# RWKV preparation of an encoder block: the next pair's k projection between the parts of a pair, the norm sums ahead of the bonus, low-rank products over 128 rows

## The chip, the cores and the metric

One core of a Trainium2 chip runs the whole kernel, one layer of a hybrid encoder block on 1024 tokens of width 1024. The metric is the device time of one execution in microseconds. The engines are TensorE (PE; its weight loads are PEld), VectorE (DVE), ScalarE (ACT) and GpSimd (POOL); SyncE (SP) issues most of the DMAs. Each engine works through its own instructions in order, and they wait for each other by semaphores.

## The reference

The block projects the normed input once, runs windowed attention and a bidirectional RWKV-7 scan on parts of the projection, joins them, and ends with an MLP and a gated embedding. The change touches only what is computed ahead of the RWKV scan:

```python
zr = proj[..., O_RWKV:O_GATE]
zr = zr + shift_mu[i] * (centred_shift(zr) - zr)
...
r, k, v = z[..., :c], z[..., c:2 * c], z[..., 2 * c:3 * c]
w_raw = (w0[:, None, None, :] + jnp.einsum('btr,drc->dbtc', jnp.tanh(wl), w2)).astype(f32)
decay = jnp.exp(-jnp.exp(-jax.nn.softplus(-w_raw) - 0.5))
a = jax.nn.sigmoid((a0[:, None, None, :] + jnp.einsum('btr,drc->dbtc', al, a2)).astype(f32))
kk = (k * k_k).astype(f32).reshape(bsz, t, *hn)
kk = kk / jnp.maximum(jnp.sqrt(jnp.sum(kk * kk, axis=-1, keepdims=True)), 1e-12)
k_dir = (k.astype(f32)[None] * (1.0 + (a - 1.0) * k_a.astype(f32))).reshape(2, bsz, t, *hn)
...
bonus = jnp.einsum('bthn,dbthn,dhn->bth', rh, k_dir, r_k.astype(f32))[..., None] * vh
```

There are 8 heads of 64, two directions d, and low ranks of 64 for w2 and a2. r, k and v each have 512 columns.

## The kernel before

**Stages.** Norm of the input and q, k, v of the attention; the RWKV preparation; then attention, the chunks of the scan, the output projection and the MLP, which this change leaves as they are. Every product in float32 is made of three matmuls of rounded parts: a high part, and a low part that is the remainder. `split` (L187, L188) makes the two: a cast on ScalarE and a subtraction on VectorE, or on GpSimd for weights. `load_w` loads 128 columns of weights in two parts (`wst`), and splits them into `whi` and `wlo`, two buffers deep.

**A pair.** The preparation goes over four pairs of heads, p = 0 to 3; a tile holds the 128 channels of a pair by all 1024 tokens. For each pair come three projections of 48 matmuls (two halves of 512 tokens, 8 blocks of k, 3 products). `shifted` evacuates one: two copies per half from PSUM on ScalarE (`zr`, `z`), a sum of the two neighbours on GpSimd (`sm`) and one operation on VectorE that ends `z`. PSUM holds two halves of a projection (`mm`, two buffers), so a third half waits for the evacuation of the first. `z` has four buffers; `zr` and `sm` have one, and `ri` shares that of `sm`.

**The norm.** `sq` is the square of k on ScalarE; `sums2` splits it and sums over a head with a matmul by a block of ones; `ri` is the larger of the sum and a small number, then Ln and Exp on ScalarE (L636, L637), each with a load of its table; `kk` is k times it. **The directions.** `lora` makes a low-rank product: two halves, each one matmul with the high weights (L547) and one with the low ones (L548), then tanh on ScalarE. The operand `lr` holds its high part in 64 rows and its low part in the other 64, so that one matmul of 128 rows does two of the three products; the low weights need only 64 rows. From the decay product come a scan over the chunks (L644), `E` and `Ei` (exponentials), `Dt`, and `ra`, half of it on GpSimd; from the rate product come `kd`, `bk` and `rk`, and `ra` and `bk` are stored. rk of the second direction times r (L680) ends a pair on VectorE. **The bonus.** `add_bonus` splits rk, transposes v on PE (`vtp`), copies it out (`vt`, L584), sums rk over the heads and multiplies by v (`bv`). It belongs to pair p, and its steps are called within pair p + 1. `vt` and `bv` share one buffer.

**What sets the order.** A scheduler at compile time orders each engine's instructions by the order of the code and a model of costs, except where `keep_in_program_order` pins one. So the code places work roughly: `proj_with` calls hooks at given matmuls (`VH`) of the v projection: before the change the rest of the last bonus and the split of sq at matmul 8, the sums of the norm at matmul 23. In the last pair `fill0` puts matmuls of the branch gates (28 or 40 at a time, `gmm`) behind the low-rank products.

Of the kernel before, what the change touches and what calls it, by code (L numbers as in the profile page):

```python
# [9 lines left out]
F32 = mybir.dt.float32  # L10
F32R = mybir.dt.float32r
AF = mybir.ActivationFunctionType
ALU = mybir.AluOpType
# [4 lines left out]
P = 128  # L18
T = 1024
# [5 lines left out]
NP = 4  # L25
NH = 8
ND = 2
FF = 4096
PLE = 256
O_RWKV = 768  # L30
# [7 lines left out]
NFS = {2: "s0", 3: "c0 s1", 4: "t0 c1 t1 s2 c2", 5: "t2 s3 c3", 6: "t3 s4 c4", 7: "s5 c5"}  # L38
EXPIN = (1, 0)
EPS_AT = (3, 3, 2, 2)  # L40
VH = (8, 23)
TPAT = (1, 3)
HDAT = (1, 4, 6)
H6 = (4, 1)
# [93 lines left out]
def block_kernel(ctx: ExitStack, tc: tile.TileContext, I: dict, out: bass.AP):  # L138
    nc = tc.nc
# [23 lines left out]
    kT_d = DR.tile([P, 2, 2, T], F32R, name="kT_d")  # L163
# [131 lines left out]
    with ExitStack() as s0:  # L295
# [141 lines left out]
        for h in range(2):  # L437
            ps = PMM.tile([P, 512], F32, name="mm", tag="mm", bufs=2)
# [21 lines left out]
    sQ.close()  # L460

    kT = PY.tile([P, 2, 2, T], F32R, name="kT", tag="yk")
    nc.gpsimd.dma_start(kT, kT_d)
    gmask = const("gmask", [P, ND, P])
    pc = G.tile([P, NPC], F32, name="pc")
    nc.sync.dma_start(pc, I["pc"])
# [9 lines left out]
    with ExitStack() as s1:  # L476
# [19 lines left out]
        nc.vector.tensor_scalar(out=oka, in0=hka, scalar1=-1.0, scalar2=1.0, op0=ALU.mult, op1=ALU.add)  # L496

        wlr_h = [A1.tile([P, ND, 512], F32R, name=f"wlrh{i}") for i in range(2)]
        wlr_l = A1.tile([P, ND, 512], F32R, name="wlrl")
        hrows, lrows = [slice(0, 64), slice(64, 128)], [slice(64, 128), slice(0, 64)]  # L500
        for i in range(2):
            st = A1.tile([P, ND, 512], F32, name="wlrst", tag="th", bufs=2)
            for rows in hrows:
                nc.sync.dma_start(st[rows], I["wa2"][hrows[i]])
            nc.vector.tensor_copy(wlr_h[i], st)
            nc.vector.tensor_tensor(out=wlr_l[hrows[i]], in0=st[hrows[i]], in1=wlr_h[i][hrows[i]].bitcast(F32), op=ALU.subtract)
        scan = A1.tile([P, T], F32, name="scan")
        nc.sync.dma_start(scan, I["scan"])

# [31 lines left out]
        def lora(d, p, i, bias_col):  # L541

            th = A1.tile([P, T], F32, name="th", bufs=2)
            for h in range(2):
                ps = PX.tile([P, 512], F32, name="px", tag="px", bufs=6)
                cs_, hs = slice(p * P, (p + 1) * P), slice(512 * h, 512 * h + 512)
                nc.tensor.matmul(ps, wlr_h[i][:, d, cs_], lr[i][:, hs], start=True, stop=False)  # L547
                nc.tensor.matmul(ps, wlr_l[hrows[i], d, cs_], lr[i][hrows[i], hs], start=False, stop=True)  # L548
                nc.scalar.activation(out=th[:, 512 * h:512 * h + 512], in_=ps, func=AF.Tanh, scale=0.5, bias=hb[:, bias_col:bias_col + 1])
            return th  # L550

# [42 lines left out]
        def fill0(p, i):  # L594

            if p == NP - 1:
                for _ in range(F0[i]):
                    next(gates0)

        def proj_with(c0, hooks):  # L600
# [9 lines left out]
                    i += 1  # L610
            return pss

        bonus = None
        for p in range(NP):
            if bonus:
                next(bonus)
            kz = shifted(O_RWKV + 512 + p * P, 4 + p)
            rz = shifted(O_RWKV + p * P, p, pin=p > 0)

            kk = A1.tile([P, T], F32, name="kk", bufs=1)  # L620
            ri = A1.tile([P, T], F32, name="ri", tag="sm", bufs=1)
# [1 line left out]
            nc.scalar.activation(out=sq, in_=kz, func=AF.Square, scale=col("k_k", p))  # L623
            sums = sums2(one_r, sq)

            def after_bonus():
                if bonus:
                    next(bonus)
                next(sums)

            def norms():
                for hs, ps in next(sums):
                    nc.vector.tensor_scalar_max(ri[:, hs], ps, 1e-24)

            vz = shifted(O_RWKV + 1024 + p * P, 8 + p, proj_with(O_RWKV + 1024 + p * P, {VH[0]: after_bonus, VH[1]: norms}), pin=True)
            nc.scalar.activation(out=ri, in_=ri, func=AF.Ln)  # L636
            nc.scalar.activation(out=ri, in_=ri, func=AF.Exp, scale=-0.5)  # L637
            nc.vector.scalar_tensor_tensor(out=kk, in0=kz, scalar=col("k_k", p), in1=ri, op0=ALU.mult, op1=ALU.mult)
            for d in range(ND):
                th = lora(d, p, 0, d * NP + p)  # L640
                fill0(p, 2 * d)
                nc.scalar.activation(out=th, in_=th, func=AF.Identity, scale=W_SCALE, bias=wsc)
                sl = slice(None) if d == 0 else slice(None, None, -1)
                nc.vector.tensor_tensor_scan(out=th[:, sl], data0=scan, data1=th[:, sl], initial=0.0, op0=ALU.mult, op1=ALU.add)  # L644
                Lc = th.rearrange("p (c t) -> p c t", t=C)
                E = A1.tile([P, NCH, C + 1], F32, name="E", bufs=1)
                Ei = A1.tile([P, NCH, C], F32, name="Ei", bufs=1)
                if d == 0:
                    nc.vector.memset(E[:, :, 0:1], 1.0)
                    E1, E2, last = E[:, :, 0:C], E[:, :, 1:C + 1], C - 1  # L650
                else:
                    nc.vector.memset(E[:, :, C:C + 1], 1.0)
                    E1, E2, last = E[:, :, 1:C + 1], E[:, :, 0:C], 0
                nc.scalar.activation(out=E2, in_=Lc, func=AF.Exp)
                nc.scalar.activation(out=Ei, in_=Lc, func=AF.Exp, scale=-1.0)
                sl = slice(None) if d == 0 else slice(None, None, -1)
                nc.vector.tensor_copy(Dt[:, d, p, sl], E2[:, :, last])
                ra = A1.tile([P, NCH, 2, C], F32, name="ra", bufs=1)
                bk = A1.tile([P, NCH, 2, C], F32, name="bk", bufs=1)

                def ch(x):
                    return x.rearrange("p (c t) -> p c t", t=C)

                nc.vector.scalar_tensor_tensor(out=ra[:, :, 0, :], in0=ch(kk), scalar=-1.0, in1=E1, op0=ALU.mult, op1=ALU.mult)
                nc.gpsimd.tensor_tensor(out=ra[:, :, 1, :], in0=ch(rz), in1=E2, op=ALU.mult)
                ta = lora(d, p, 1, 8 + d * NP + p)
                fill0(p, 2 * d + 1)
                kd = A1.tile([P, T], F32, name="kd", bufs=1)
                nc.scalar.activation(out=kd, in_=ta, func=AF.Identity, scale=hka[:, p:p + 1], bias=oka[:, p:p + 1])
                nc.vector.tensor_tensor(out=kd, in0=kd, in1=kz, op=ALU.mult)  # L670
                nc.vector.scalar_tensor_tensor(out=ta, in0=ta, scalar=1.0, in1=kk, op0=ALU.add, op1=ALU.mult)
                bs, ks = (0, 1) if d == 0 else (1, 0)
                nc.vector.scalar_tensor_tensor(out=bk[:, :, bs, :], in0=ch(ta), scalar=0.5, in1=Ei, op0=ALU.mult, op1=ALU.mult)
                nc.vector.tensor_tensor(out=bk[:, :, ks, :], in0=ch(kd), in1=Ei, op=ALU.mult)
                if d == 0:
                    rk = A1.tile([P, T], F32, name="rk", bufs=1)
                    nc.vector.tensor_scalar_mul(rk, kd, col("r_k", p))
                else:
                    nc.vector.scalar_tensor_tensor(out=rk, in0=kd, scalar=col("r_k", NP + p), in1=rk, op0=ALU.mult, op1=ALU.add)
                    nc.vector.tensor_tensor(out=rk, in0=rk, in1=rz, op=ALU.mult)  # L680
                nc.sync.dma_start(ra_d[d, :, :, p, :].rearrange("c q x -> q c x"), ra.rearrange("q c a t -> q c (a t)"))
                nc.sync.dma_start(bk_d[d, :, :, p, :].rearrange("c q x -> q c x"), bk.rearrange("q c a t -> q c (a t)"))
            bonus = add_bonus(p, rk, vz)

        fill0(NP - 1, 4)
        for _ in bonus:
# [1107 lines left out]
```

## Time and profile before

| | |
|---|---|
| median of 3 runs | 1844.6 us (1842.85 to 1845.58) |
| the profiled execution | 1840.7 us |
| its span, first to last instruction | 1838.9 us |
| PE busy | 1726.5 us, 94% |
| VectorE busy | 1135.0 us, 62% |
| ScalarE busy | 880.4 us, 48% |
| GpSimd busy | 322.2 us, 18% |
| mean granted TensorE clock | 0.977 |
| the preparation's projections, k of pair 0 on PE | from 123.5 us |
| last rk product (L680) of pairs 0, 1, 2, 3 ends at | 201.6, 251.3, 301.8, 356.4 us |
| first attention scores on PE (L839) | 384.8 us |

A busy PE is not a PE at its peak: matmuls are pipelined, and one of 512 columns lasts 0.39 us while the next starts 0.23 us behind it. In rows of the timeline stand the start, the length, engine, line, operation, output and inputs; in square brackets stands how long the engine was idle before it, and what ended that. The share of the whole span says little of one stage, so the preparation is cut out by times.

### The profile page before, as it was taken

To read this page: it belongs to the slowest core of one execution; us is meant where nothing else is said; L and a number is where in the kernel's file an instruction comes from. 1 tells how busy PE (TensorE), PEld (TensorE's weight loads), DVE (VectorE), ACT (ScalarE), POOL (GpSimd) and SP (SyncE) were. 2 spreads that over 40 slices of the span, in tenths; PEclk is the share of its full clock that TensorE was granted. 3 is DMA by queue.
4 is the path that set the end of the run, shared out by engine and by line. 5 is a ranking of instruction groups with operands and counts; after the bars stand their busy time and mean duration, and the time that the engine had idled before them with its cause. 6 is when DMAs were issued, how large, how long until landed. Compare 5 with 4: busy or idle time off the path is not lost. (4 is left out here: it accounts for less than half of the span.)

```text
span 1838.9 us, 31199 instructions
## 1 busy us (share of the span) xinstructions
PE 1726.5 (94%) x12056; PEld 1414.7 (77%) x12056; DVE 1135.0 (62%) x1947; ACT 880.4 (48%) x1640; POOL 322.2 (18%) x265
## 2 busy tenths in 40 slices
PE   7999888999999899988889989999999999999998
PEld 7976666666677777776669978777877888888998
DVE  5645777745936555676563487666675777685432
ACT  5545666547754545556531245444343444554221
POOL 3453544531132121121132000000000000000000
PEclk9998999999999999999999989999999999999999
DMA  5462344674377474676564315544546874564111
GB/s 200 99 175 92 103 143 144 194 204 115 100 206 206 128 211 130 176 216 191 180 209 155 104 40 181 163 132 144 165 132 226 297 255 121 189 218 141 56 40 41
DMA packets 287125, 286.06 MB, mean 156 GB/s; under 512 B 49409, under 2 KB 203905, under 8 KB 286849
## 3 DMA queue, kind: packets, MB, share of 16 engines
q1 hardware_dynamic: 278720, 270.76, 47.7%
q0 software_dynamic: 7824, 12.59, 2.5%
q8 instruction: 95, 1.56, 0.4%
q10 hardware_dynamic: 432, 0.73, 0.1%
q14 instruction: 54, 0.43, 0.1%
HBM read 203.26 MB, written 80.74 MB: 154 GB/s over the span
## 5 line engine op out<-in xcount | busy, mean ns | idle before, releaser
L188 POOL TENSOR_TENSOR wlo<-wst,whi 128x512 fp32r<-128x512 f32 (+1 forms) x108 | 170.1, 1588 | 341.1 <-ACT whi L187 296.8
L1681 PE MATMUL ff2ps<-th,sh 128*128 128x512 f32 x448 | 174.2, 391 | 4.1 <-ACT th L187 4.1
L1681 PE MATMUL ff2ps<-tl,sh 128*128 128x512 f32 x448 | 175.0, 391 | 0.0
L1681 PE MATMUL ff2ps<-th,sl 128*128 128x512 f32 x448 | 174.9, 390 | 0.0
L175 POOL TENSOR_TENSOR rstd<-ms,neghalf 128x1 f32<-128x1 f32 x24 | 13.3, 554 | 813.8 <-DVE ms L173 813.8
L187 ACT CAST sh<-sst 128x512 fp32r<-128x512 f32 x109 | 67.8, 622 | 114.9 <-PE ff2ps L1681 72.0
L188 DVE TENSOR_TENSOR sl<-sst,sh 128x512 fp32r<-128x512 f32 x109 | 75.0, 688 | 52.5 <-ACT sh L187 52.3
L1681 PEld LDWEIGHTS ff2ps<-th,sh 128*128 128x128 f32 x448 | 84.2, 188 | 22.3 <-ACT th L187 4.5
L1681 PEld LDWEIGHTS ff2ps<-th,sl 128*128 128x128 f32 x448 | 84.5, 189 | 17.7
L1681 PEld LDWEIGHTS ff2ps<-tl,sh 128*128 128x128 f32 x448 | 84.5, 189 | 17.5
L187 ACT CAST whi<-wst 128x512 fp32r<-128x512 f32 (+1 forms) x108 | 68.9, 650 | 57.0 <-DMA wst<-in_w_in_dram 17.4
L187 ACT CAST w1h<-w1st 128x512 fp32r<-128x512 f32 x48 | 29.2, 614 | 102.3 <-DMA w1st<-in_w_ff_dram 101.7
L226 PE MATMUL plps<-wg,hp 128*128 128x256 f32 x256 | 73.5, 287 | 0.0
L228 PE MATMUL plps<-wg,hp 128*128 128x256 f32 x256 | 72.5, 283 | 0.0
L226 PE MATMUL mmo<-whi,mh 128*128 128x256 f32 x256 | 72.4, 283 | 0.0
L227 PE MATMUL plps<-wg,hp 128*128 128x256 f32 x256 | 72.4, 283 | 0.0
L228 PE MATMUL mmo<-whi,ml 128*128 128x256 f32 x256 | 72.1, 282 | 0.0
L227 PE MATMUL mmo<-wlo,mh 128*128 128x256 f32 x256 | 72.1, 282 | 0.0
L188 DVE TENSOR_TENSOR w1l<-w1st,w1h 128x512 fp32r<-128x512 f32 x48 | 32.7, 686 | 52.7 <-ACT w1h L187 52.7
L208 PE MATMUL gps<-rm,bkp 128*128 128x256 f32 x256 | 62.1, 385 | 2.3 <-ACT tm L1061 1.5
L1034 DVE TENSOR_TENSOR gm<-gps,gmask 128x512 f32<-128x512 f32 x64 | 43.7, 684 | 29.5 <-PE gps L208 29.5
L1757 ACT ACTIVATE pth<-plps 128x256 f32<-128x256 f32 x32 | 12.3, 385 | 101.6 <-PE plps L228 101.6
(399 smaller groups left out, 5190.4 us busy)
## 6 DMA issues: line engine op xcount, KB each, us to landing
wst<-in_w_in_dram SPq DMA_DIRECT2D x92, 256.0 KB, 3.6
tst<-in_w_ff_dram SPq DMA_DIRECT2D x80, 256.0 KB, 3.9
w1st<-in_w_ff_dram SPq DMA_DIRECT2D x32, 512.0 KB, 5.5
hid_S<-h SPq DMA_DIRECT2D x64, 256.0 KB, 2.1
sst<-hid_S SPq DMA_DIRECT2D x64, 256.0 KB, 2.7
hid_A<-h SPq DMA_DIRECT2D x48, 256.0 KB, 2.0
sst<-hid_A SPq DMA_DIRECT2D x45, 256.0 KB, 3.7
ra_d<-ra SPq DMA_DIRECT2D x8, 1024.0 KB, 4.5
```

Source lines behind the costliest of these rows:

```text
L175: nc.gpsimd.tensor_tensor(out=r, in0=ms, in1=neghalf.broadcast_to([P, width]), op=ALU.pow)
L187: a = nc.scalar.copy(hi, src)
L188: b = (lo_eng or nc.vector).tensor_tensor(out=lo, in0=src, in1=hi.bitcast(F32), op=ALU.subtract)
L208: tc.keep_in_program_order(nc.tensor.matmul(*a, **kw))
L226: nc.tensor.matmul(ps, ah, bh, start=(i == 0), stop=False)
L227: nc.tensor.matmul(ps, ah, bl, start=False, stop=False)
L228: nc.tensor.matmul(ps, al, bh, start=False, stop=(i == n - 1))
L1034: nc.vector.tensor_tensor(out=gm[d][:, s % NB, 4 * h:4 * h + 4, :], in0=ps.rearrange("p j q t -> p (j q) t"), in1=gmask[:, d, :].unsqueeze ...
L1681: nc.tensor.matmul(banks[bs][i], x_[:, isl], y_, start=fresh and p + j == 0, stop=p == NPR - 1 and j == 2, skip_group_check=True)
L1757: nc.scalar.activation(out=th[:, 256 * m:256 * m + 256], in_=ps_, func=AF.Tanh, scale=0.5)
```

## The change

1. **Order.** The k projection of pair p + 1 (`k_of`) is called between the decay product of direction 0 and its scan; its r projection (`r_of`) at the end of pair p. Before, both opened pair p + 1.
2. **Hooks.** In the v projection the split of sq comes at matmul 2 and the norm's sums at 18; the split of rk comes at 20 and the rest of the bonus at 38.
3. **Low-rank products.** Each of the two operands gets low weights of its own with 128 rows, of which 64 are filled with zeros on GpSimd (the high weights times 0). L548 becomes a matmul of 128 rows.
4. **Buffers.** `rk` takes the buffer of `vt` and `bv`. The load of kT on GpSimd's queue is called in pair 1 instead of ahead of the preparation.

```diff
-VH = (8, 23)
+VH = (2, 18, 20, 38)
...
     kT = PY.tile([P, 2, 2, T], F32R, name="kT", tag="yk")
-    nc.gpsimd.dma_start(kT, kT_d)
...
-        wlr_l = A1.tile([P, ND, 512], F32R, name="wlrl")
+        wlr_l = [A1.tile([P, ND, 512], F32R, name=f"wlrl{i}") for i in range(2)]
...
             nc.vector.tensor_copy(wlr_h[i], st)
-            nc.vector.tensor_tensor(out=wlr_l[hrows[i]], in0=st[hrows[i]], in1=wlr_h[i][hrows[i]].bitcast(F32), op=ALU.subtract)
+
+            nc.gpsimd.tensor_scalar_mul(wlr_l[i][lrows[i]], wlr_h[i][lrows[i]].bitcast(F32), 0.0)
+            nc.vector.tensor_tensor(out=wlr_l[i][hrows[i]], in0=st[hrows[i]], in1=wlr_h[i][hrows[i]].bitcast(F32), op=ALU.subtract)
...
-                nc.tensor.matmul(ps, wlr_l[hrows[i], d, cs_], lr[i][hrows[i], hs], start=False, stop=True)
+                nc.tensor.matmul(ps, wlr_l[i][:, d, cs_], lr[i][:, hs], start=False, stop=True)
...
+        def k_of(p):
+            return shifted(O_RWKV + 512 + p * P, 4 + p)
+
+        def r_of(p):
+            return shifted(O_RWKV + p * P, p)
+
         bonus = None
+        kz, rz = k_of(0), r_of(0)
         for p in range(NP):
-            if bonus:
-                next(bonus)
-            kz = shifted(O_RWKV + 512 + p * P, 4 + p)
-            rz = shifted(O_RWKV + p * P, p, pin=p > 0)
+            nkz = None
...
-            def after_bonus():
-                if bonus:
-                    next(bonus)
-                next(sums)
+            def step(g):
+                if g:
+                    next(g)
...
-            vz = shifted(O_RWKV + 1024 + p * P, 8 + p, proj_with(O_RWKV + 1024 + p * P, {VH[0]: after_bonus, VH[1]: norms}), pin=True)
+            vz = shifted(O_RWKV + 1024 + p * P, 8 + p, proj_with(O_RWKV + 1024 + p * P, {
+                VH[0]: lambda: next(sums), VH[1]: norms, VH[2]: lambda: step(bonus), VH[3]: lambda: step(bonus)}))
+            if p == 1:
+                nc.gpsimd.dma_start(kT, kT_d)
...
                 th = lora(d, p, 0, d * NP + p)
+                if p + 1 < NP:
+                    if d == 0:
+                        nkz = k_of(p + 1)
                 fill0(p, 2 * d)
...
-                    rk = A1.tile([P, T], F32, name="rk", bufs=1)
+                    rk = A1.tile([P, T], F32, name="rk", tag="vt", bufs=1)
...
             bonus = add_bonus(p, rk, vz)
+            if p + 1 < NP:
+                kz, rz = nkz, r_of(p + 1)
```

The scheduler makes of it the following. Rows are instructions in an engine's order; lines of the changed program lie some lines further down than those of before (L680 became L690, L644 became L654).

VectorE, from the end of pair 1 (the last product of rk with r, first row) to kk of pair 2, before the change; `s` and `s2l` are the low halves of a split, `z` is what `shifted` ends, `px` a sum in PSUM:

```order
L680 TENSOR_TENSOR rk<-rk,z 128x1024
L649 MEMSET E 128x16
L188 TENSOR_TENSOR s_1408<-rk,s_1408 128x512
L188 TENSOR_TENSOR s2l<-rk,s2h 128x512
L523 SCALAR_TENSOR_TENSOR z<-sm,hmu,z 128x1024
L513 MEMSET zr 128x1
L514 MEMSET zr 128x1
L188 TENSOR_TENSOR s_1408<-sq,s_1408 128x512
L188 TENSOR_TENSOR s2l<-sq,s2h 128x512
L588 TENSOR_TENSOR bv<-px,z 128x512 x2
L633 TENSOR_SCALAR ri<-px 128x512 x2
L638 SCALAR_TENSOR_TENSOR kk<-z,pc,ri 128x1024
```

The same stretch after the change, and two rows further:

```order
L690 TENSOR_TENSOR rk<-rk,z 128x1024
L188 TENSOR_TENSOR s_1410<-sq,s_1410 128x512
L188 TENSOR_TENSOR s2l<-sq,s2h 128x512
L514 MEMSET zr 128x1
L637 TENSOR_SCALAR ri<-px 128x512 x2
L188 TENSOR_TENSOR s_1410<-rk,s_1410 128x512
L188 TENSOR_TENSOR s2l<-rk,s2h 128x512
L515 MEMSET zr 128x1
L659 MEMSET E 128x16
L645 SCALAR_TENSOR_TENSOR kk<-z,pc,ri 128x1024
L524 SCALAR_TENSOR_TENSOR z<-sm,hmu,z 128x1024
L589 TENSOR_TENSOR bv<-px,z 128x512 x2
```

The halves of sq and ri now stand ahead of the halves of rk, `bv` stands behind kk and the z of v, ahead of the scan, and the z that stood between the halves (of r) has moved to the end of the pair.

VectorE behind the first scan of pair 2, before:

```order
L644 SCALAR_TENSOR_TENSOR th<-scan,th 128x1024
L670 TENSOR_TENSOR kd<-kd,z 128x1024
L657 COPY Dt<-E 128x16
L664 SCALAR_TENSOR_TENSOR ra<-kk,E 128x16x64
L671 SCALAR_TENSOR_TENSOR th<-th,kk 128x1024
```

and after:

```order
L654 SCALAR_TENSOR_TENSOR th<-scan,th 128x1024
L667 COPY Dt<-E 128x16
L674 SCALAR_TENSOR_TENSOR ra<-kk,E 128x16x64
L662 MEMSET E 128x16
L524 SCALAR_TENSOR_TENSOR z<-sm,hmu,z 128x1024
L514 MEMSET zr 128x1
L515 MEMSET zr 128x1
L680 TENSOR_TENSOR kd<-kd,z 128x1024
```

The z of the next pair's k (fifth row) now stands ahead of kd and all that follows; on GpSimd the sum that it reads stands behind that engine's half of `ra` and one `wlo`.

ScalarE at the norm, before:

```order
L517 COPY zr<-mm 128x512
L520 ACTIVATE z<-mm,omm 128x512
L636 ACT_TABLE_LOAD
L636 ACTIVATE ri<-ri 128x1024
L637 ACT_TABLE_LOAD
L637 ACTIVATE ri<-ri 128x1024
```

and after:

```order
L518 COPY zr<-mm 128x512
L521 ACTIVATE z<-mm,omm 128x512
L187 CAST s_1410<-rk 128x512
L187 CAST s2h<-rk 128x512
L643 ACT_TABLE_LOAD
L643 ACTIVATE ri<-ri 128x1024
L585 COPY vt<-vtp 128x512 x2
L644 ACT_TABLE_LOAD
L644 ACTIVATE ri<-ri 128x1024
```

The casts of rk and the two copies of v's transposes moved into the norm; the copies read what PE transposes 7 matmuls behind the low sums of the norm. Elsewhere: PE has, per pair, the v projection with 4 + 4 sums and 8 transposes, 4 low-rank matmuls, the next k, the other 12 low-rank matmuls, the next r. The matmuls with the low parts of sq stand 13 matmuls behind those with the high parts. GpSimd issues the load of kT at the same place as before, ahead of the first sum of the preparation, and the two fills with zeros stand behind it, each ahead of one of the first two sums. Behind the preparation every engine's order is the same as before.

## The prediction

> **What bounds the kernel now.** The change touches one stage, the RWKV preparation, so I cut the span by its pairs of heads: from the end of one pair's last rk product on VectorE (L680) to the next. The view of windows gives pairs 1, 2 and 3, and a stretch that is used further down.
>
> ```profile
> 201.55:251.33 49.78, 44.76 (x176) 33.24 (x176) 37.59 (x37) 32.07 (x46) 23.10 (x11) 0.97 0.45 137
> 251.33:301.77 50.44, 45.65 (x176) 33.78 (x176) 37.66 (x38) 32.11 (x47) 23.13 (x11) 0.93 0.45 136
> 301.77:356.39 54.62, 51.96 (x198) 38.69 (x199) 39.46 (x33) 34.70 (x51) 29.55 (x17) 0.94 0.52 157
> 168.00:176.00 8.00, 8.00 (x16) 4.66 (x16) 8.00 (x8) 3.42 (x4) 6.13 (x2) 0.50 0.11 33
> ```
>
> After each length stand the busy us (and counts) of PE, PEld, DVE, ACT and POOL, then granted clock, DMA share and GB/s. PE is busy 45 of 50 us and looks like the bound, but part of that is half clock. The other view, VectorE in order of time, shows a chain that closes on itself.
>
> ```profile
> 250.12 1.21 DVE L680 TENSOR_TENSOR rk<-rk,z 128x1024 f32<-128x1024 f32 x1
> ...
> 252.40 2.02 DVE L188 TENSOR_TENSOR s<-rk,s 128x512 fp32r<-128x512 f32 x1 [1.03 <-ACT s L187]
> 254.34 0.68 DVE L188 TENSOR_TENSOR s2l<-rk,s2h 128x512 fp32r<-128x512 f32 x1
> ...
> 257.82 1.29 DVE L588 TENSOR_TENSOR bv<-px,z 128x512 f32<-128x512 f32 x2 [0.39 <-DMA v_d<-vt]
> 261.73 1.29 DVE L633 TENSOR_SCALAR ri<-px 128x512 f32<-128x512 f32 x2 [2.62 <-PE px L570]
> 267.04 1.28 DVE L638 SCALAR_TENSOR_TENSOR kk<-z,pc,ri 128x1024 f32<-128x1024 f32 x1 [4.03 <-ACT ri L637]
> 271.35 1.29 DVE L523 SCALAR_TENSOR_TENSOR z<-sm,hmu,z 128x1024 f32<-128x1024 f32 x1 [3.02 <-POOL sm L522]
> 272.56 2.29 DVE L644 TENSOR_TENSOR_SCAN th<-scan,th 128x1024 f32<-128x1024 f32 x1
> ...
> 274.77 2.25 DVE L670 TENSOR_TENSOR kd<-kd,z 128x1024 f32<-128x1024 f32 x1
> 276.94 2.15 DVE L657 COPY Dt<-E 128x16 f32<-128x16 f32 x1
> 279.01 1.21 DVE L664 SCALAR_TENSOR_TENSOR ra<-kk,E 128x1024 f32<-128x1024 f32 x1
> 280.15 1.21 DVE L671 SCALAR_TENSOR_TENSOR th<-th,kk 128x1024 f32<-128x1024 f32 x1
> ...
> 284.22 2.28 DVE L644 TENSOR_TENSOR_SCAN th<-scan,th 128x1024 f32<-128x1024 f32 x1
> ...
> 288.23 3.19 DVE L670 TENSOR_TENSOR kd<-kd,z 128x1024 f32<-128x1024 f32 x1 [1.70 <-ACT E L654]
> ...
> 300.56 1.21 DVE L680 TENSOR_TENSOR rk<-rk,z 128x1024 f32<-128x1024 f32 x1
> ```
>
> VectorE sits idle almost only between L680 and the scan, where the norm is made: PE's sums (2.62), Ln and Exp (4.03), the sum of shifts on GpSimd (3.02). From 271 to 301 it waits once. So a pair has two parts: end of L680 (251.33) to end of the first scan (274.85), 23.5 us, mostly latency; and from there to the next L680 (301.77), 26.9 us, nearly solid VectorE work. The change reorders that ring, and I count it again in the new order.
>
> **First part, new order.** ScalarE's two steps, the three GpSimd groups and the memset come from these views (activities in order of time, one line's group, groups by form):
>
> ```profile
> 262.28 1.28 ACT L636 ACT_TABLE_LOAD   x1
> 263.58 1.06 ACT L636 ACTIVATE ri<-ri 128x1024 f32<-128x1024 f32 x1
> ```
> ```profile
> L584 ACT COPY vt<-vtp x8: 576/584/603, 203.5 to 366.1; 128x512 f32<-128x512 f32 x8
> ```
> ```profile
> L188 POOL TENSOR_TENSOR wlo<-wst,whi 128x512 fp32r<-128x512 f32 x43 | 74.8, 1749 | 85.9 <-ACT whi L187 85.9
> L522 POOL TENSOR_TENSOR sm<-zr 128x1024 f32<-128x1024 f32 x14 | 27.2, 1946 | 53.5 <-ACT zr L517 26.8 <-issue 25.4 <-DVE zr L514 1.3
> L665 POOL TENSOR_TENSOR ra<-z,E 128x1024 f32<-128x1024 f32 x8 | 21.1, 2633 | 0.6
> L792 POOL MEMSET rm<- 128x1024 f32 x2 | 1.9, 960 | 0.1
> ```
>
> Clock zero is the end of L680. The norm's two low halves come first, 0.68 each, end 1.3; the last low matmul and the two maxima bring ri to 2.65. The bonus's low halves, bv and one z have left this stretch: that is the gain, since ri ended 11.7 after L680 before (263.02 against 251.33). Then ScalarE: the copy of v's first half, two casts of rk and a table load end near 3.2, Ln 4.25. Now the two vt copies stand between Ln and the second table load; they need PE's 7 matmuls and 8 transposes after the low sums, and end at 5.4. Table load 6.7, Exp 7.8, kk 9.1. The gap of 3.02 to z stays (whi cast, wlo, then the sum of shifts), z ends 13.4. The bonus product bv now stands ahead of the scan: 14.7. The scan ends at 17.0, against 23.5: **−6.5**. bv's wait for the v_d store (0.39 above) is covered: vt ends at 5.4 and bv begins at 13.4.
>
> **Second part.** Here the order costs. z of the next k stands ahead of kd. After the scan: E on ScalarE, about 1 us (Ln of the same columns: 1.06), Dt and ra 3.2 (276.94 to 280.15), so VectorE is free at 21.2. But GpSimd begins its ra only at 18.0 and needs 2.63 + 1.75 + 1.95 (ra, wlo, sum of shifts) to 24.4: a new wait of **3.2 us**. z ends 25.6, kd 27.8 (2.17 from start to start), the next four steps 4.07 (280.15 to 284.22), second scan 34.1. From there the old path took 15.3 us (286.5 to 301.77) with a 1.70 wait for E which goes, since kd no longer stands behind it: 13.6. L680 ends at **47.7**, against 49.8 and 50.4: −2.1 and −2.7. The next k projection must have left PE by about 21; it starts at 8 and takes 48 matmuls at 0.23, so 19.3: hidden by 2 us. On SP the weight loads now alternate with the stores; the tightest is r's second part behind the v_d store at 5.4:
>
> ```profile
> wst<-in_w_in_dram SPq DMA_DIRECT2D x92, 256.0 KB, 3.6
> ```
>
> With 3.6 us to landing it is there at 9, and ScalarE casts it at about 11: hidden.
>
> **The clock.** In the new order PE waits about 3 us for PSUM at the head of the v projection (r's first half is evacuated only after both exponentials), and about 3 us again at the low sums, which wait for L680.
>
> ```profile
> 252.42 0.79 PE L569 MATMUL px<-s,one_r 128*128 128x512 f32 x1 [3.51 <-ACT s L187]
> ```
>
> After a wait of 3.51 us the next matmul took 0.79, half clock. If that happens at the low sums, the 7 matmuls and 8 transposes (1.6 + 1.0) double, and Exp, kk and all behind come 2.6 later; if not, 0. Two waits of three each are near the observed size and neither is above it, so I take half, **+1.3**: pairs of 49.0, −0.8 and −1.4, together −2.2. The Trainium skill ("TensorE: Matmul & The Clock Gate", Part 1) puts the drop to half at an idle window of about 3.4 us; by that rule neither wait would do it and the sum would be 2.6 us lower for the two pairs. The 0.50 clock in the fourth window row, with PE busy 8.00 of 8.00, speaks against idle time as the only cause.
>
> **Pair 3** has no next k, so the second part keeps its order and only the first part's gain counts.
>
> ```profile
> 324.36 2.28 DVE L644 TENSOR_TENSOR_SCAN th<-scan,th 128x1024 f32<-128x1024 f32 x1
> ```
>
> The scan ended 24.9 after L680 and will end at 18.3: **−6.6**. The low-rank products change there too:
>
> ```profile
> 271.83 0.50 PE L548 MATMUL px<-lr,wlrl 64*128 64x512 f32 x1
> 272.26 0.51 PE L226 MATMUL mm<-hh,whi 128*128 128x512 f32 x1
> 272.61 0.39 PE L227 MATMUL mm<-hl,whi 128*128 128x512 f32 x1
> 272.84 0.39 PE L228 MATMUL mm<-hh,wlo 128*128 128x512 f32 x1
> ```
>
> Around a 64-row matmul starts are 0.43 and 0.35 apart, among 128-row ones 0.23. Sixteen per pair save about 3 us of PE. In pairs 0 to 2 this lies beside VectorE and is worth nothing unless PE becomes the bound; in pair 3 the low-rank products come earlier past the gate matmuls, and I take **−1** (bounds 0 and −3). The Trainium skill (same page, "Why this matters for your kernels") says a single matmul of few rows takes as long as one of 128; by that rule alone this term is 0. The rows above differ from it.
>
> **Pair 0.** Two fills with zeros are new on GpSimd, priced between the memset (0.96) and the sum of shifts (1.95). The second waits for a cast that VectorE makes late and stands ahead of a sum of shifts, so the copy that frees PSUM for r comes about 3 us later:
>
> ```profile
> 135.81 0.50 PE L226 MATMUL mm<-hh,whi 128*128 128x512 f32 x1 [1.11 <-ACT z L520]
> ```
>
> That wait of 1.11 grows to about 4, but r's second half then waits less behind it; what remains is the risk of half clock. With k's z in the second part against the old stalls of this pair I take **+1** (−1 to +3.5).
>
> **Tail.** rk now shares vt's buffer, so the last vt copies wait for rk's low half. Between pairs PE covers this; at the end nothing does: **+1** (0 to +4, the upper end if the gate weights, which have less time then, come late). The load of kT costs nothing: it stands where it stood in GpSimd's order.
>
> **Sum:** +1 − 2.2 − 6.6 − 1 + 1 = −7.8. All behind the preparation is the same on every engine and hangs on it, so I carry the shift to the end. The profiled execution took 1840.7 us (span 1838.9), the median of the runs is 1844.6; −7.8 of the one gives 1832.9, and beside the median **1836.5** or so, which I predict.
>
> **Rivals.** (a) *Given back* (within 0.2%, that is ±3.7 us, about what a measurement of this kernel can tell from no change): half clock in every pair (+2.6 where I took 1.3), pair 0 at +3.5 and the tail at +3: −7.8 + 3.9 + 2.5 + 2 = +0.6, 1845. For it: 0.79 after 3.51. Against: three bad ends at once. 0.19. (b) *Slower*: z of the next k holds VectorE's queue in pairs 0 to 2. If half clock lasts 12 us from the low sums on (8 us of it in a row stand in the fourth window), PE is done 6 us late, at 25, and each us past 21 delays kd, both scans and L680. At +4 in three pairs the time is −7.8 + 12 = +4, 1849. It decides from about 2 us of lateness, 4 us of half clock. Against it: mean clocks of 0.97 and 0.93 over 50 us are 3 and 7 us at half, and that with two waits in a row. 0.11. (c) *PE-bound*: no half clock and the GpSimd leg shorter than its means, so PE's own 40 us and one wait set the pair at 42 to 43: −7 per pair, −9 in pair 3, about 1821. Against it: the ring above needs 47.7. 0.06. (d) *It does not do what it says*: the norm sums' low halves were sorted 13 matmuls behind the high ones, and kT did not move. The first costs nothing while L680 is later than both; this is inside the forecast.
>
> **Numbers.** Forecast 0.64, from 1827 (full clock, −1 more per pair by a kd of 1.2, pair 3 at −10, pair 0 at −1, no tail) to 1841. Above it stand (a) and part of (b): the range is 1827 to 1846. Faster 0.70, same 0.19, slower 0.11.
>
> **What would show it.** Right: L680 to L680 at 47 to 50; the wait before ri under 1 us; a wait of about 3 for GpSimd's sum before k's z; vt between Ln and Exp; pair 3's first scan 17 to 20 after L680. Wrong: a wait of kd or k's z for PE, half clock beyond 5 us, or the last gate matmuls of the stage shifted by less than L680 of pair 3.

## The result and the profile after

| | before | after |
|---|---|---|
| median, both kernels on the same chip | 1845.1 us (1838.3 to 1851.2, 8 runs) | 1855.4 us (1849.0 to 1861.2, 8 runs) |
| after to before | | 1.0066, 95% interval 1.0043 to 1.0088 |
| span of the profiled execution | 1838.9 us | 1855.9 us |

Forecast was 8 us faster; the kernel is about 12 us slower. The stretch from one pair's last rk product (now L690) to the next is read from the view of windows, with the columns as in the prediction: pairs 1, 2 and 3, and at last the 5 us in which pair 0's r projection begins.

```profile
213.28:264.74 51.46, 43.52 (x176) 34.45 (x176) 39.12 (x39) 32.18 (x45) 24.09 (x11) 0.93 0.44 133
264.74:316.17 51.43, 43.49 (x176) 34.38 (x176) 39.20 (x39) 32.19 (x45) 24.08 (x11) 0.93 0.44 133
316.17:367.08 50.91, 46.81 (x194) 36.60 (x195) 39.70 (x32) 30.21 (x43) 24.63 (x14) 0.97 0.54 164
144.90:150.00 5.10, 5.02 (x12) 3.96 (x13) 3.99 (x5) 2.14 (x4) 4.12 (x3) 0.50 0.36 103
```

Against the rows of before (49.78, 50.44, 54.62), pairs 1 and 2 have grown by 1.7 and 1.0, and pair 3 has shrunk by 3.7. Pair 0's last rk product ends at 213.3 instead of 201.5: 11.8 late. The first attention score starts at 393.9 instead of 384.8, so the tail behind pair 3 has shrunk by 1.6. The sum is +11.8 + 1.7 + 1.0 − 3.7 − 1.6 = +9.2, and 393.9 − 384.8 = 9.1: the loss stands in pair 0, and of the gain expected in the pairs only a part of pair 3's came. The rest of the 17 us between the two spans lies behind the preparation, where the instructions are the same in the same order; the medians differ by 10.3.

Pair 0 first. The rows of the timeline of after are from TensorE, ScalarE, GpSimd and VectorE, where the r projection should begin:

```profile
144.98 0.79 PE L226 MATMUL mm<-hh,whi 128*128 128x512 f32 x1 [9.66 <-ACT z L521]
```
```profile
143.75 0.59 ACT L518 COPY zr<-mm 128x512 f32<-128x512 f32 x1 [5.59 <-POOL sm L523]
```
```profile
126.35 2.78 POOL L506 TENSOR_SCALAR wlrl<-wlrh 64x1024 fp32r<-64x1024 f32 x1
...
135.25 3.26 POOL L506 TENSOR_SCALAR wlrl<-wlrh 64x1024 fp32r<-64x1024 f32 x1 [0.64 <-DVE wlrh L504]
141.82 1.89 POOL L523 TENSOR_TENSOR sm<-zr 128x1024 f32<-128x1024 f32 x1 [3.32 <-DVE zr L515]
```
```profile
137.89 1.17 DVE L534 CAST lr<-z 64x1024 fp32r<-64x1024 f32 x1
139.08 2.45 DVE L535 TENSOR_TENSOR lr<-z,lr 64x1024 fp32r<-64x1024 f32 x2
141.58 0.06 DVE L514 MEMSET zr<- 128x1 f32 x1
141.59 0.06 DVE L515 MEMSET zr<- 128x1 f32 x1
```

And before, from GpSimd and VectorE:

```profile
132.37 2.17 POOL L522 TENSOR_TENSOR sm<-zr 128x1024 f32<-128x1024 f32 x1 [1.29 <-DVE zr L514]
```
```profile
132.12 0.06 DVE L513 MEMSET zr<- 128x1 f32 x1
...
132.83 2.27 DVE L533 CAST lr<-z 64x1024 fp32r<-64x1024 f32 x1
```

Read it backwards. PE stands still for 9.66 us at the r projection (before: 1.11), because ScalarE has not emptied the first half of k out of PSUM. ScalarE waits for a sum of shifts on GpSimd, which reads the one `zr` buffer. That sum starts at 141.82 instead of 132.37, 9.45 late. For 6.1 of it GpSimd itself is busy longer: the two fills take 2.78 and 3.26, a `wlo` takes longer, and the second fill, which also waits for its cast, ends only at 138.51. For the other 3.32 the sum waits for nothing but two memsets of one column, 0.06 us each, that clear the edges of `zr`. They stand in VectorE's queue behind the splits of `lr`; before, they stood ahead of them (132.12). After the wait PE runs at half clock for 5 us (last window row: 0.50). The first scan of pair 0 starts at 178.50 instead of 168.09: 10.4 of the 11.8.

Now the pairs. VectorE and then GpSimd behind the second scan of pair 1, in after:

```profile
247.26 2.28 DVE L654 TENSOR_TENSOR_SCAN th<-scan,th 128x1024 f32<-128x1024 f32 x1
249.47 1.20 DVE L680 TENSOR_TENSOR kd<-kd,z 128x1024 f32<-128x1024 f32 x1
250.67 0.17 DVE L667 COPY Dt<-E 128x16 f32<-128x16 f32 x1
250.75 1.22 DVE L674 SCALAR_TENSOR_TENSOR ra<-kk,E 128x1024 f32<-128x1024 f32 x1
251.89 3.22 DVE L681 SCALAR_TENSOR_TENSOR th<-th,kk 128x1024 f32<-128x1024 f32 x1
255.03 2.91 DVE L684 TENSOR_TENSOR bk<-kd,Ei 128x1024 f32<-128x1024 f32 x1
257.87 2.31 DVE L683 SCALAR_TENSOR_TENSOR bk<-th,Ei 128x1024 f32<-128x1024 f32 x1
260.10 2.31 DVE L689 SCALAR_TENSOR_TENSOR rk<-kd,pc,rk 128x1024 f32<-128x1024 f32 x1
...
263.53 1.21 DVE L690 TENSOR_TENSOR rk<-rk,z 128x1024 f32<-128x1024 f32 x1
```
```profile
250.77 3.26 POOL L675 TENSOR_TENSOR ra<-z,E 128x1024 f32<-128x1024 f32 x1 [8.57 <-DVE kd L680]
253.98 2.89 POOL L523 TENSOR_TENSOR sm<-zr 128x1024 f32<-128x1024 f32 x1
256.83 4.50 POOL L188 TENSOR_TENSOR wlo<-wst,whi 128x512 fp32r<-128x512 f32 x2
```

VectorE waits for no releaser here, and yet four operations of about 1.2 us take 2.3 to 3.2. The ends tell why. GpSimd's `ra` ends at 254.03, and VectorE's L681 ends at 255.11, 1.1 later. GpSimd's sum ends at 256.87, and L684 ends at 257.94, again 1.1 later; the next two end as far behind the two `wlo`. Each engine's operation seems to do its work only when the other's is over, so GpSimd's time is added to VectorE's. The Trainium skill ("SBUF — State Buffer", Who interferes with whom) says that a VectorE instruction with two SBUF inputs and a GpSimd instruction that reads SBUF exclude each other for the whole instruction; these four rows agree with it. Before, r's sum of shifts ran beside the scan and a wait of VectorE for ScalarE; in the new order it stands in the middle of solid VectorE work. From GpSimd, before:

```profile
235.63 2.11 POOL L522 TENSOR_TENSOR sm<-zr 128x1024 f32<-128x1024 f32 x1 [7.01 <-issue]
```

The first part is late as well: from the end of L690 (213.28) to the end of the first scan (232.24) it takes 18.96.

```profile
226.53 2.30 DVE L524 SCALAR_TENSOR_TENSOR z<-sm,hmu,z 128x1024 f32<-128x1024 f32 x1 [3.04 <-POOL sm L523]
```

VectorE's wait for v's sum of shifts is there as forecast (3.04), and z itself takes 2.30, beside a `wlo`. Half clock is there too: after a wait of 3.48 us PE is granted 0.50 from 215.0 to 218.4, at the norm's sums.

### The profile page after: what moved, and what is told of

It is laid out like the page before. It is cut to its first block, busy times and chain, and to the rows that moved or that the text cites. A ratio compares the mean times of both kernels' runs of the same rounds, so it can differ in the third digit from the quotient of the medians.

```text
span 1855.9 us, 31204 instructions
## 1 busy us (share of the span) xinstructions
PE 1723.5 (93%) x12056; PEld 1423.5 (77%) x12056; DVE 1142.2 (62%) x1947; ACT 879.9 (47%) x1640; POOL 329.6 (18%) x267
## 5 line engine op out<-in xcount | busy, mean ns | idle before, releaser
L188 DVE TENSOR_TENSOR sl<-sst,sh 128x512 fp32r<-128x512 f32 x109 | 75.1, 689 | 53.6 <-ACT sh L187 53.3
L188 DVE TENSOR_TENSOR w1l<-w1st,w1h 128x512 fp32r<-128x512 f32 x48 | 32.7, 686 | 51.6 <-ACT w1h L187 51.6
L218 PE MATMUL gmm<-hh,wlo 128*128 128x512 f32 x144 | 59.3, 412 | 1.9 <-POOL wlo L188 1.9
```

What stands on the lines that cost most here:

```text
L188: b = (lo_eng or nc.vector).tensor_tensor(out=lo, in0=src, in1=hi.bitcast(F32), op=ALU.subtract)
L218: mm(ps, al, bh, start=False, stop=(i == n - 1))
```

## The experiments

Each is compared with the kernel before on the same chip: the first number is the ratio of its time to that, with the 95% interval. Scans and pairs come from one profiled execution each; a pair is counted here from the start of one last rk product to the start of the next (before: 49.8, 50.4 and 53.6 for pairs 1 to 3; after: 51.5, 51.4 and 49.9).

Runs 1 to 4 ask where the loss comes from. **Theory of the start:** the fills and what they do to the queues ahead of pair 0's first scan. **Rival:** the new order of the pairs.

**1. The order alone.** The changed kernel with low-rank products of 64 rows as before, so without fills.

```diff
-                nc.tensor.matmul(ps, wlr_l[i][:, d, cs_], lr[i][:, hs], start=False, stop=True)
+                nc.tensor.matmul(ps, wlr_l[hrows[i], d, cs_], lr[i][hrows[i], hs], start=False, stop=True)
```

> The changed kernel with its low-rank products as before: low weights of 64 rows, no fills with zeros; order, hooks and buffers of pairs as changed. Start theory (the loss is made before pair 0's first scan, where the fills on GpSimd and the late clearing of zr's edges hold PE for 9.7 us): pair 0's rk product (L690 of the changed kernel) ends at 201 to 204 us instead of 213.3, the wait of 9.66 at the head of r falls to 1 to 3, the time comes to within 0.3% of the kernel before (ratio 0.998 to 1.003). Pair theory (the loss is made in the new order of pairs): the time stays 8 to 14 us above before, ratio 1.004 to 1.008.

1.0014 (0.9997 to 1.0031). PE's waits at the start are 0.99 and 2.27, and the first scan starts at 170.1, not 178.5. The start is most of the way back, but pairs 1 and 2 take 53.3 and 51.6: the order alone gains nothing.

**2. The products alone.** The kernel before with products of 128 rows and the fills; rk takes the buffer of vt to make room.

```diff
-            nc.vector.tensor_tensor(out=wlr_l[hrows[i]], in0=st[hrows[i]], in1=wlr_h[i][hrows[i]].bitcast(F32), op=ALU.subtract)
+            nc.gpsimd.tensor_scalar_mul(wlr_l[i][lrows[i]], wlr_h[i][lrows[i]].bitcast(F32), 0.0)
+            nc.vector.tensor_tensor(out=wlr_l[i][hrows[i]], in0=st[hrows[i]], in1=wlr_h[i][hrows[i]].bitcast(F32), op=ALU.subtract)
```

> The kernel before with the products of 128 rows and the two fills alone (rk in the buffer of vt and bv, for room). Start theory: the same wait of 8 to 10 us at the head of r in pair 0, pair 0's rk product ends 8 to 11 us late, pairs 1 and 2 as before within 1 us, pair 3 up to 3 us shorter; slower by 5 to 11 us, ratio 1.003 to 1.006. Pair theory: as fast as before or faster by up to 5 us, ratio 0.997 to 1.001.

1.0045 (1.0024 to 1.0066). The old order, and PE waits at the same place:

```profile
145.59 0.79 PE L226 MATMUL mm<-hh,whi 128*128 128x512 f32 x1 [10.01 <-ACT z L522]
```

So the wait at the start comes with the fills, in the old order as in the new. Two expectations failed: the first scan of pair 0 starts 8.1 us late, but its last rk product only 3.9 (8 to 11 were expected), and pairs 1 to 3 take 52.0, 51.6 and 55.0, each 1.2 to 2.1 longer than before, where 1 at most and in pair 3 a gain was expected.

**3. A fill that waits for nothing.** The changed kernel, its low weights cleared whole by an early memset.

```diff
+        for i in range(2):
+            nc.gpsimd.memset(wlr_l[i].bitcast(F32), 0.0)
...
-            nc.gpsimd.tensor_scalar_mul(wlr_l[i][lrows[i]], wlr_h[i][lrows[i]].bitcast(F32), 0.0)
```

> The changed kernel, its low weights cleared whole by a GpSimd memset ahead of the loads, which waits for no cast. Start theory: the wait at the head of r falls from 9.7 to 1 to 5 us, pair 0's rk product ends 5 to 11 us earlier, the time is 5 to 11 us below the changed kernel (ratio to before 0.999 to 1.003). If the fills' own time and not their wait for the cast is the cause: less than 3 us of gain. Pair theory: no gain beyond 3 us.

0.9994 (0.9976 to 1.0013). PE has no wait above 2 us between 120 and 152 us, and the first scan starts at 164.9: the start is mended, and 3 us better than before; in this trace the first sum of shifts stands ahead of the load of kT (118.93, and 126.69 before). Pairs 1 and 2 stay at 51.4 and 51.3.

**4. The edges off VectorE's queue.** The changed kernel, fills and all, with the edges of zr cleared on GpSimd, right ahead of the sum that reads them.

```diff
-            nc.vector.memset(zr[:, 0:1], 0.0)
-            nc.vector.memset(zr[:, T + 1:T + 2], 0.0)
+            nc.gpsimd.memset(zr[:, 0:1], 0.0)
+            nc.gpsimd.memset(zr[:, T + 1:T + 2], 0.0)
```

> The changed kernel with the edges of zr cleared on GpSimd instead of VectorE, so that the sum of shifts no longer waits behind VectorE's casts and low halves; the fills stay. If the clearing in VectorE's queue is the greater part: the wait at the head of r falls by 4 to 7 us and the time with it. If the fill with its wait for the cast is: it falls by less than 3 us.

0.9992 (0.9972 to 1.0011). The fills are still there, and PE's wait falls from 9.66 to 3.67:

```profile
138.29 0.50 PE L226 MATMUL mm<-hh,whi 128*128 128x512 f32 x1 [3.67 <-ACT z L521]
```

This does not price the memsets alone, for the scheduler changed GpSimd's order with them:

```profile
134.69 2.34 POOL L523 TENSOR_TENSOR sm<-zr 128x1024 f32<-128x1024 f32 x1
137.00 3.20 POOL L506 TENSOR_SCALAR wlrl<-wlrh 64x1024 fp32r<-64x1024 f32 x1
```

The second fill now stands behind the sum of shifts, where in after it stood ahead. The sum starts 7.1 earlier than in after: 3.3 of that is the wait for the memsets, and 3.8 is the fill that left its path. The pairs change too: 49.3 and 48.2. That made a second theory: the same memsets lengthen every pair.

**5. Both mends**, the diffs of 3 and 4 together.

> The changed kernel with the low weights cleared whole at the start (no wait for the cast) and the edges of zr cleared on GpSimd, both. Start theory (the loss stands ahead of pair 0's first scan, and the clearing in VectorE's queue is what carries it): no wait of PE above 2.5 us between 120 and 152 us, first scan of pair 0 by 166, as with the early fill alone (164.87). Pair theory (the clearing also sits between a projection and its sum of shifts in every pair, worth 2 to 3 us a pair: pairs were 49.3, 48.2 and 48.0 with the edges on GpSimd against 51.4): pairs 1 and 2 under 49.5, first attention score by 375, ratio 0.994 to 0.997. Rival (the two mends take away the same thing): pairs as with the early fill alone, 51 and more, ratio 0.998 to 1.000.

0.9959 (0.9942 to 0.9975): 0.4% faster than the kernel before. Pairs of 49.2, 49.5 and 47.8, so the two mends take away different things; the first score at 379.7 missed its 375. With all edges on GpSimd pair 0's first sum of shifts stands behind the load of kT again (127.51), its first scan starts at 168.0, not by 166, and its last rk product ends at 203.9, where run 3 has 199.6. The windows of pairs 1 to 3, and VectorE's z of v in pair 2 with GpSimd's sum:

```profile
203.87:253.04 49.17, 43.18 (x176) 34.45 (x176) 38.20 (x32) 32.21 (x45) 24.59 (x17) 0.93 0.46 139
253.04:302.57 49.53, 43.36 (x176) 34.56 (x176) 38.09 (x33) 32.31 (x45) 24.49 (x17) 0.93 0.45 138
302.57:351.36 48.79, 42.59 (x172) 32.37 (x173) 36.86 (x29) 29.95 (x42) 22.31 (x13) 0.96 0.52 160
```
```profile
261.95 1.28 DVE L646 SCALAR_TENSOR_TENSOR kk<-z,pc,ri 128x1024 f32<-128x1024 f32 x1 [5.22 <-ACT ri L645]
265.34 1.28 DVE L525 SCALAR_TENSOR_TENSOR z<-sm,hmu,z 128x1024 f32<-128x1024 f32 x1 [2.10 <-POOL sm L524]
```
```profile
263.41 1.89 POOL L524 TENSOR_TENSOR sm<-zr 128x1024 f32<-128x1024 f32 x1 [14.97 <-DVE kk L646]
```

kk starts 8.9 us after the last rk product in both kernels (253.04 to 261.95 here, 264.74 to 273.65 in after). What differs lies behind it: in after a `wlo` stands ahead of the sum of shifts and another beside z; here the sum comes first. The wait falls from 3.04 to 2.10 and z from 2.30 to 1.28: 2 us. So the second theory came out right in its size and not in its cause: in pairs 1 to 3 of after no sum waits for a memset, and what moving them changed is the order that the scheduler gave GpSimd's queue.

**6. The edges in the kernel before.** The diff of 4 on the old order.

> The kernel before, with nothing but the edges of zr cleared on GpSimd. If the clearing hurts because of the new order alone: pairs of 49 to 50.5 and 54 as before, ratio 0.999 to 1.001. If it held the old order back as well: pairs shorter by 1 to 3 us each, ratio 0.995 to 0.998.

1.0004 (0.9988 to 1.0020), pairs of 54.2, 51.4 and 54.1 with pair 0 6 us earlier. It is no gain of its own. That pair 1 came out at 54.2 was expected by neither; TensorE ran at half clock there from 216.4 to 226.6, and the second scan waited 3.58 us for ScalarE.

**7. Both mends, with k at the pair's end.**

```diff
-                if p + 1 < NP:
-                    if d == 0:
-                        nkz = k_of(p + 1)
...
-                kz, rz = nkz, r_of(p + 1)
+                kz, rz = k_of(p + 1), r_of(p + 1)
```

> Both mends, with the next pair's k projection called at the end of a pair, ahead of r: the new hooks and the 128-row products without the early k. If the early k is worth what the second part was forecast to lose and the first to gain: the norm waits for k again, first scan 4 us or more later behind the last rk product of the pair before, pairs 1 and 2 at 51 to 53 against 48 to 49.5, ratio 3 to 8 us above the kernel with both mends. If the hooks carry it all: pairs within 0.5 us of that kernel's.

1.0019 (1.0001 to 1.0038); pairs of 52.3, 51.8 and 54.5. The first scan of pair 1 ends 25.5 us after the rk product (198.62 to 224.10), against 16.7 in run 5. The early k is worth 3.1, 2.3 and 6.6 us.

**8. Both mends, with the old hooks.**

```diff
-VH = (2, 18, 20, 38)
+VH = (1, 8, 23)
...
-                VH[0]: lambda: next(sums), VH[1]: norms, VH[2]: lambda: step(bonus), VH[3]: lambda: step(bonus)}))
+                VH[0]: lambda: step(bonus), VH[1]: lambda: (step(bonus), next(sums)), VH[2]: norms}))
```

> Both mends and the early k, with the old order in the v projection: split of rk at matmul 1, the rest of the bonus and the split of sq at 8, the sums at 23. If the hooks carry the first part (ri 2.65 instead of 11.7 us after the last rk product): first scan 3 us or more later in pairs 1 to 3, pairs 1 and 2 at 51 to 53. If the early k carries it: pairs within 0.5 us of the kernel with both mends.

1.0039 (1.0023 to 1.0056); pairs of 54.6, 52.8 and 46.4. The first scan of pair 1 ends 21.1 us after the rk product, 4.4 later than in run 5; in pair 3 only 2.3 later. Pair 3 is short because gate matmuls are left over: 139 of them stand behind the last rk product, and 92 in run 5, and the first score comes 41.9 us behind it, and 28.3 in run 5. Neither half of the new order gains without the other.

**9. The mended order with products of 64 rows**: the diffs of 1 and 4.

> The new order with the edges of zr on GpSimd and the low-rank products of 64 rows as before, so no fills at all. If the 128-row products are worth what the prediction took (nothing in pairs 0 to 2, 1 us in pair 3, bounds 0 and 3): pairs 1 and 2 within 0.5 us of those with both mends (49.2 and 49.5), pair 3 up to 3 us longer than 47.8, ratio 0.996 to 0.998. Rival (the mixing of 64 and 128 rows makes PE late, so that k's z and kd wait): pairs longer by 1 us or more, as 53.3 and 51.6 without the edges, ratio 0.999 to 1.003.

1.0014 (0.9995 to 1.0033): the rival. Pairs of 53.4, 51.1 and 48.6. Two places of its pair 1, TensorE's twelve low-rank matmuls behind the next k, and what VectorE waits for after the second scan:

```profile
227.26 0.40 PE L546 MATMUL px<-lr,wlrh 128*128 128x512 f32 x1
227.59 0.50 PE L547 MATMUL px<-lr,wlrl 64*128 64x512 f32 x1
...
233.31 0.79 PE L226 MATMUL mm<-hh,whi 128*128 128x512 f32 x1
```
```profile
244.29 1.23 DVE L678 TENSOR_TENSOR kd<-kd,z 128x1024 f32<-128x1024 f32 x1 [3.42 <-ACT kd L677]
```

The twelve take 6.05 us (227.26 to 233.31), and the clock drops to half among them (0.50 from 230.8 on), with no wait ahead of it. In run 5 they take 2.73:

```profile
223.99 0.39 PE L549 MATMUL px<-lr,wlrh 128*128 128x512 f32 x1
224.22 0.40 PE L550 MATMUL px<-lr,wlrl 128*128 128x512 f32 x1
...
226.72 0.39 PE L226 MATMUL mm<-hh,whi 128*128 128x512 f32 x1
```

Behind them stands the r projection, and on ScalarE the copy of r's first half stands ahead of direction 1's tanh; so a late PE reaches kd, and VectorE waits 3.42.

**10. The old order with 128 rows and the early memset**: the diffs of 2 and 3.

> The old order with products of 128 rows whose low weights are cleared by an early memset: the products without the loss at the start. By the prediction: pairs 0 to 2 as before (49.8 and 50.4 within 0.5), pair 3 shorter by 1 (0 to 3), ratio 0.998 to 1.000. Rival, a cost of its own: ratio above 1.002, as the 1.0045 with the late fills. If that 1.0045 came from the fills alone, the start is back here: first scan of pair 0 at 168 or earlier.

1.0028 (1.0009 to 1.0046), and it doesn't separate what it was meant to. The memset came behind the load of kT on GpSimd, VectorE waited 5.56 us for it, and PE still waited 7.91 at r; the first scan starts at 174.2, not by 168. No fill stands between its first two sums of shifts, and yet the second waits for the two memsets, which stand behind the splits of `lr` in VectorE's late queue:

```profile
141.04 1.89 POOL L525 TENSOR_TENSOR sm<-zr 128x1024 f32<-128x1024 f32 x1 [5.17 <-DVE zr L517]
```

Pairs of 51.6, 51.4 and 54.9 are 1 to 2 longer than before, where nothing or a gain of 1 was expected.

**11. GpSimd's half of ra on VectorE**, beside both mends.

```diff
-                nc.gpsimd.tensor_tensor(out=ra[:, :, 1, :], in0=ch(rz), in1=E2, op=ALU.mult)
+                nc.vector.tensor_tensor(out=ra[:, :, 1, :], in0=ch(rz), in1=E2, op=ALU.mult)
```

> Both mends, and GpSimd's half of ra given to VectorE: 8 more operations of 1.21 us there, 8 of 2.2 us fewer on GpSimd. Theory (VectorE's operations beside GpSimd's last 2.2 to 3.2 instead of 1.2 us, and k's z waits 2.8 us for a sum that stands behind ra): the stretch comes back, ra of VectorE 1.21 instead of 3.2 in direction 0, z's wait under 1.5; second scan to last rk product 0.5 to 1.5 us shorter, pairs of 47 to 48.5, ratio 0.990 to 0.995. Rival (VectorE's time is the same wherever the work is done): pairs 1 to 2.4 us longer, 50.5 to 52, ratio 0.998 to 1.002.

0.9950 (0.9932 to 0.9969). VectorE behind the first scan of pair 1 in run 5, and here:

```profile
221.74 3.24 DVE L675 SCALAR_TENSOR_TENSOR ra<-kk,E 128x1024 f32<-128x1024 f32 x1
...
228.00 1.28 DVE L525 SCALAR_TENSOR_TENSOR z<-sm,hmu,z 128x1024 f32<-128x1024 f32 x1 [2.81 <-POOL sm L524]
```
```profile
221.85 1.23 DVE L675 SCALAR_TENSOR_TENSOR ra<-kk,E 128x1024 f32<-128x1024 f32 x1
222.99 1.22 DVE L676 TENSOR_TENSOR ra<-z,E 128x1024 f32<-128x1024 f32 x1
...
227.25 1.29 DVE L525 SCALAR_TENSOR_TENSOR z<-sm,hmu,z 128x1024 f32<-128x1024 f32 x1 [2.89 <-POOL sm L524]
```

With GpSimd's operation gone, the same instruction takes 1.23 instead of 3.24, and both halves on VectorE (2.36) are 0.9 us shorter than one beside GpSimd. From the second scan's end to the last rk product it is 14.4 instead of 15.25, with an operation more. The forecast of a shorter wait for k's z failed (2.89): a `wlo` that waits for its cast stands there too. Pairs are 49.8, 48.2 and 48.6, two longer and one shorter than in run 5, and the intervals of the two ratios lie over each other.

**12. The first edges on VectorE, the rest on GpSimd**, beside both mends.

```diff
+            edge = nc.vector if mi in (0, 4, 8, 12, 13) else nc.gpsimd
+            edge.memset(zr[:, 0:1], 0.0)
+            edge.memset(zr[:, T + 1:T + 2], 0.0)
```

> Both mends, with the edges of the first projections (the two low-rank ones and k, r, v of pair 0) cleared on VectorE as with the early fill alone, all others on GpSimd. Pair 0 as with the early fill alone (first scan 164.9, last rk product 198.4), pairs of 49.2, 49.5 and 47.8 as with both mends: last rk product of pair 3 at 345 against 349.2, ratio 0.993 to 0.995. Rival (the start's gain is given back in pair 1, where the second projection is late): no earlier than 348.5.

0.9955 (0.9936 to 0.9975). The last rk product starts at 198.8 in pair 0 and at 344.3 in pair 3 (345 expected), and the pairs are 48.2, 49.5 and 47.8. The trace does what was said; the gain of 5 us over run 5 at the first score (374.7) doesn't show in the ratio.

## Why the prediction was wrong

**Pair 0: +1 forecast, +11.8 measured.** This is the step that failed: 10.8 of the 17 us between −7.8 and +9.2 are here. "That wait of 1.11 grows to about 4, but r's second half then waits less behind it; what remains is the risk of half clock" counted the fills on GpSimd alone, and too short: about 3 us, from 0.96 to 1.95 for a fill, where the fills took 2.78 and 3.26 and with the rest of GpSimd's queue made the sum of shifts 6.1 late. The chain PE, ScalarE, GpSimd was right, and it was not followed one step further, into VectorE's queue, where the edges' memsets had moved behind the splits of lr: the other 3.3. The wait grew to 9.66, not to about 4, and the half clock named as a risk came (0.50 in the last window row). That the fills bring this is shown: without them (run 1) or with an early one (run 3) the wait is 2.3 or less, and with them in the old order (run 2) it is 10.01. How it divides into 6.1 and 3.3 is read from the trace of after; no run takes away one alone.

**Pairs 1 and 2: 49.0 forecast, 51.46 and 51.43 measured.** By the prediction's own three pieces, in pair 1: first part 18.3 with half clock against 18.96; from there to the second scan's end 17.1 against 17.3; to L690 13.6 against 15.2. The mechanism was right, and the wait of 3.2 for k's z was there (2.82). Two terms were off. The last piece took away the old wait of 1.70 for E and left the rest as it was, without asking what GpSimd would now do beside it: a sum of shifts, 1.89 long when alone, came into it, and the piece is 1.6 longer. And in the first part, 17.0 at full clock, half clock put kk at 8.9 instead of 7.8 and a `wlo` beside z added 1.0; without that `wlo`, in run 5, it is 16.65. The two waits of PE that the prediction put at about 3 were 4.26 and 3.48 around the end of pair 0, and half clock followed each for 3.4 us.

**Pair 3: −7.6 forecast, −3.7 measured.** The first scan ends 19.1 us after L690 (18.3 forecast, 24.9 before), so −5.8 of the −6.6 arrived; the two pieces behind it, forecast to shrink by 1 in all, grew by 1 us each, in both beside a `wlo` (L687 takes 1.78 instead of 0.74 before, L689 2.29 instead of 1.27). **Tail: +1 forecast, −1.6 measured**, outside its bounds of 0 and +4; rk in vt's buffer cost nothing there that shows.

**The products.** "Worth nothing unless PE becomes the bound" in pairs 0 to 2 was wrong for the new order: run 9 against run 5 gives 4.2, 1.5 and 0.7 us in pairs 1 to 3. PE needn't be the bound of a pair for its lateness to count; it is enough that ScalarE's queue puts its output ahead of something that VectorE needs. In run 9 the matmuls of 64 and 128 rows in turn start 0.33 to 0.43 us apart at full clock, in run 5 those of 128 rows 0.23, and half clock makes up the rest of 6.05 against 2.73. The Trainium skill ("TensorE: Matmul & The Clock Gate", Why this matters for your kernels) says of a single matmul of few rows that it takes as long as one of 128; where the two alternate, the traces differ from it.

**The rivals.** None of them was this. The slower one was to come from k's z that waits for PE; in pair 1 that wait is for GpSimd, 2.82 long, and not for PE:

```profile
239.76 1.29 DVE L524 SCALAR_TENSOR_TENSOR z<-sm,hmu,z 128x1024 f32<-128x1024 f32 x1 [2.82 <-POOL sm L523]
```

The forecast's own size was there to be had once the queues were mended: 0.9959 in run 5.

**What stays open.** Run 3 puts the first score 4.7 us ahead of the kernel before, and its ratio is 0.9994; run 12 puts it 10 ahead and its ratio is 0.9955. A shift at the first score isn't carried whole to the end, and the runs don't show where the rest goes. Why the old order with 128 rows has longer pairs (runs 2 and 10) wasn't separated from the shared buffer of rk; in pair 1 of run 10 the copies of `vt` wait 2.21 us for rk's low half, where before they wait for nothing. The change also takes the `pin` off the projections of r and v, which leaves their order to the scheduler; no run puts it back.

## What to carry to other kernels

Follow a wait to its last link: an instruction of 0.06 us in the wrong queue held three engines here (3.3 us in after, 5.2 in run 10), so when an edit adds work on one engine, look for what the scheduler has moved in the queues of the others. Work on GpSimd isn't free beside a full VectorE: count its own length, in the stretch where it lands. When an experiment moves one instruction, look at what the scheduler moved with it before giving that instruction the credit, as run 4 shows. Price a change of order together with its mates: here, with the queues mended, leaving out the early k, the hooks or the 128-row products turned 0.4% of gain into none.

## What the runs showed of the hardware

GpSimd and VectorE take turns: the same 128x1024 operation of VectorE on two SBUF inputs takes 1.22 us alone and up to 3.24 beside GpSimd, ending 1.1 us after GpSimd's. GpSimd's tensor_scalar over 64x1024 takes 2.78 us, where its memset of 128x1024 took 0.96 in the prediction's row. Half clock needs no long wait. In run 5 the v projection began after 2.46 us and slowed at its sixth matmul; in run 9 it set in among the twelve, with PE busy for 20 us ahead of it:

```profile
240.46 0.50 PE L214 MATMUL mm<-hh,whi 128*128 128x512 f32 x1 [2.46 <-ACT z L522]
...
241.72 0.61 PE L218 MATMUL mm<-hh,wlo 128*128 128x512 f32 x1
```
```profile
230.15 0.50 PE L547 MATMUL px<-lr,wlrl 64*128 64x512 f32 x1
230.58 0.63 PE L546 MATMUL px<-lr,wlrh 128*128 128x512 f32 x1
231.14 0.79 PE L547 MATMUL px<-lr,wlrl 64*128 64x512 f32 x1
```

The Trainium skill's idle window of about 3.4 us ("TensorE: Matmul & The Clock Gate", Part 1) doesn't cover the second. The traces tie it to the 64-row matmuls. In the fourteen traces half clock sets in five times between 120 and 375 us with PE busy for the 6.8 us ahead of it: in before (166.9), run 1 (232.2), run 6 (216.4 and 271.0) and run 9 (230.8). All are kernels with products of 64 rows, and each time four or five of these stand, in turn with those of 128 rows, in the last 4 us; in the ten traces with products of 128 rows it never happens. The first of them is the half clock with PE busy in the prediction's fourth window row.
